# One block on one core: the output projection's second half reordered, the second norm's vectors loaded as columns, the planner's prices changed

## The chip, the cores and the metric

The kernel runs on 1 core of one Trainium2 chip. The metric is the device time of one execution in microseconds (us). Engines are named as in the profile: PE (TensorE, matrix products), DVE (VectorE), ACT (ScalarE), POOL (GpSimd), SP (SyncE, which here only issues transfers). Each engine runs its own list of instructions strictly in the order of the program, so an instruction that waits also holds everything behind it on that engine.

## What is computed

The reference is one block of an encoder on 512 rows of 1024 numbers, all in float32. Cut to what matters here:

```python
mod = silu(c) @ w_ada + b_ada
sh1, sc1, g1, sh2, sc2, g2 = split(mod, 6)
h = rms(x, norm1_g) * (1 + sc1) + sh1
z = h @ w_in                                   # 33 pieces of 128 columns
rec = hgrn2(...)                               # 4 recurrent heads of 128
att = dsa_attention(...)                       # 8 heads of 64: four pairs, 128 wide each
mix = concat([rec, att]) @ w_out               # the output projection, 1024 x 1024
x = x + g1 * mix
h2 = rms(x, norm2_g) * (1 + sc2) + sh2
logits = h2 @ [w_rg, w_re] + [b_rg, b_re]      # 20 columns: 4 groups, 16 experts
# each row goes to 2 of 16 experts: y = (silu(h2 @ w1) * (h2 @ w3)) @ w2
x = x + g2 * y
```

## The kernel before

A product of two float32 matrices is done as three products of split numbers: each operand is split into a high part (`wh`, `hx[..][:, 0]`) and a low part (`wl`), and `mm3` issues high by high, high by low, low by high. ACT casts the high part of each weight piece, and DVE (now and then POOL) subtracts it to get the low part.

**The planner.** The first part of the program, up to the experts, is not written in the order in which it runs. Every piece of work is a generator that is handed to `Desk` with a rank. The desk keeps an estimated clock for each engine, takes the generator that can begin first (in steps of 100 ns, then by rank), and lets it issue. `Engine.call` gives the estimated price of each instruction. So the prices set the order in which each engine's list is written. On the chip only that order is left: the estimates themselves delay nothing.

**The stages.** (1) `square_gen` squares the four pieces `xt` of x on ACT and adds them up on DVE in one sum `acc`; one float32 product with a matrix of ones gives the sums of squares of the first norm. `norm1_gen` multiplies eight chunks of w_ada by silu(c) for its vectors. (2) The 33 pieces of z are computed (`z_gen`) beside the recurrent heads, the indexer with its top-256 search (`topk_gen`), the four head pairs of attention (`attend_gen(j)`, j = 0 to 3), and the other six parts of mod: `ada_gen` goes through 64 loads `dd` in eight groups, sums each group on DVE (`acc`), turns it on PE and writes 512 numbers to the scratch `modD` in HBM. (3) `out_gen` is the output projection: half 0 takes the recurrent heads (tiles `mix` 0 to 3), half 1 the head pairs (`mix` 4 to 7). For each half there are two column halves c, four row tiles t, and per (c, t) two weight pieces p of two head tiles each, so 12 products per (c, t), 96 per half. The results stand in two PSUM banks of tag `z`. Half 1 begins only when all four head pairs are done; at that point the tiles of the attention are freed (`gp.close()`), the pool `mw` is opened in their place, and weight piece `NZ + 5` (half 1, c = 0, p = 1) is split into it. (4) `post_gen(t)` turns each finished row tile `xm[t]`, multiplies it by the router's weights `wr`, picks the experts and stores h2. `rows_gen` prepares the second norm: it loads sh2 and sc2 from `modD` as rows that are repeated on all 128 partitions (`sh2b`, `gs2b`), turns them on PE to columns (`shT`, `gsT`) and folds them into `wr` and the bias `cb`. (5) The 16 experts follow in an order that is written by hand: 12 weight pieces of 512 KB per expert come through a ring of 34 places, are split on ACT and DVE, and used on PE. SP issues their loads in order, each as soon as its place is free; the first eight wait for the end of `ada_gen`, since they use its memory.

In the names of the profile, `a`, `z`, `o`, `u` are PSUM banks, `nl` is an attention tile, `csm` holds the constant matrix of the head norm, and nearly every instruction has line L177, that of the planner's helper.

## Time and profile before

| | |
|---|---|
| median of 3 runs | 728.02 us (727.63 to 729.42) |
| the profiled execution | 727.48 us |
| its span, first to last instruction | 725.6 us |
| PE busy | 683.1 us (94%) |
| DVE busy | 630.9 us (87%) |
| ACT busy | 439.0 us (61%) |
| mean granted TensorE clock | 0.987 |

A busy PE in this profile is not a PE at its peak, since products overlap and their ends are modelled. The chain of work that ended last runs half of its time through PE, 21% through transfers and 14% through DVE. Times in the text are us from the start of the span.

### The profile page before, as it was taken

How to read it: one execution, taken by the hardware profiler on the slowest of the kernel's cores; microseconds unless marked ns; L12 is line 12 of the kernel's file. 1: busy time of each engine (PE TensorE's matmuls, PEld its weight loads, DVE VectorE, ACT ScalarE, POOL GpSimd, SP SyncE). 2: the span in 40 equal slices, each digit the busy share in tenths (PEclk: the TensorE clock that was granted, in tenths of full speed). 3: DMA queues.
4: the chain of work that ended last, by engine and by line, in shares of the span. 5: the costliest groups of instructions: out<-in, count | busy, mean ns of one | idle time of the engine just before them, and what ended most of it. 6: DMA issues, size and time to landing. Idle time of an engine off the chain costs nothing.

```text
span 725.6 us, 10941 instructions
## 1 busy us (share of the span) xinstructions
PE 683.1 (94%) x3794; PEld 530.9 (73%) x3794; DVE 630.9 (87%) x1057; ACT 439.0 (61%) x670; POOL 202.4 (28%) x104
## 2 busy tenths in 40 slices
PE   3999999999999999999889979999999999999993
PEld 1666778877778776667568858888888888888872
DVE  4637889999999987978866889999999999999991
ACT  4326664545557466553343458888777777777770
POOL 0120010001321321122200030165655655556412
PEclk9999999999999999999989999999999999999997
DMA  9947532231120324685697889999999999999502
GB/s 363 406 154 224 190 111 88 89 115 59 56 90 30 117 88 164 225 308 181 188 362 305 315 318 406 390 376 347 365 363 367 354 350 358 364 361 349 187 11 33
DMA packets 57388, 172.84 MB, mean 238 GB/s; under 512 B 11954, under 2 KB 12530, under 8 KB 56304
## 3 DMA queue, kind: packets, MB, share of 16 engines
q1 hardware_dynamic: 45168, 150.54, 56.1%
q0 software_dynamic: 10720, 17.24, 8.5%
q10 hardware_dynamic: 1440, 4.31, 1.5%
q8 instruction: 32, 0.52, 0.3%
q14 instruction: 28, 0.23, 0.1%
HBM read 167.50 MB, written 15.24 MB: 252 GB/s over the span
## 4 chain that ended last, share of the span: by engine, by line
PE 50%; DMA 21%; DVE 14%; issue 10%; ACT 3%; SPq 0%; POOL 0%; POOLq 0%; DVEq 0%; ACTq 0%
PE z L177 30%; PE a L177 14%; DMA w<-in_w_dram 13%; DVE wl L177 8%; DMA out_dram<-yo,idx 6%; PE u L177 2%; PE h L177 2%; PE o L177 2%; DMA dd<-in_w_ada_dram 1%; DMA chunk<-in_w_ada_dram 1%; DVE yo L177 1%; DVE xl L177 1%; DVE oh L177 1%; ACT wh L177 1%; ACT sq L177 1%
## 5 line engine op out<-in xcount | busy, mean ns | idle before, releaser
L177 ACT CAST wh<-w 128x1024 fp32r<-128x1024 f32 x168 | 174.5, 1054 | 44.2 <-PE h L177 30.9
L177 DVE TENSOR_TENSOR wl<-w,wh 128x1024 fp32r<-128x1024 f32 x168 | 196.6, 1216 | 2.4 <-ACT wh L177 2.0
L177 PE MATMUL z<-hx,wh 128*128 128x512 f32 x496 | 163.1, 409 | 1.1 <-DVE hx L177 0.6
L1358 POOL DMA_INDIRECT out_dram<-yo,idx x16 | 123.7, 7730 | 120.8 <-DVE wl L177 64.1
L177 PEld LDWEIGHTS z<-hx,wh 128*128 128x128 f32 x496 | 88.8, 189 | 27.1 <-issue 8.7
L177 PE MATMUL h<-wl,xh 128*128 128x512 f32 x256 | 101.4, 396 | 0.0
L177 PE MATMUL h<-wh,xh 128*128 128x512 f32 x256 | 100.8, 394 | 0.0
L177 PE MATMUL h<-wh,xl 128*128 128x512 f32 x256 | 100.6, 393 | 0.0
L177 ACT CAST wh<-raw 128x1024 fp32r<-128x1024 f32 x64 | 67.1, 1052 | 55.3 <-PE z L177 48.0
L177 PE MATMUL z<-hx,wl 128*128 128x512 f32 x248 | 97.6, 394 | 0.0
L177 DVE TENSOR_TENSOR wl<-raw,wh 128x1024 fp32r<-128x1024 f32 x64 | 81.6, 1286 | 6.8 <-ACT wh L177 6.5
L177 PEld LDWEIGHTS h<-wl,xh 128*128 128x128 f32 x256 | 48.5, 189 | 12.9 <-DVE wl L177 3.0
L177 PEld LDWEIGHTS h<-wh,xh 128*128 128x128 f32 x256 | 48.5, 189 | 10.2
L177 PEld LDWEIGHTS h<-wh,xl 128*128 128x128 f32 x256 | 48.4, 189 | 10.1 <-DVE xl L177 0.3
L177 PE MATMUL y<-wh,hh 128*128 128x512 f32 x128 | 53.0, 414 | 2.0 <-DVE yo L177 2.0
L177 PEld LDWEIGHTS z<-hx,wl 128*128 128x128 f32 x248 | 46.8, 189 | 10.3
L177 PE MATMUL y<-wl,hh 128*128 128x512 f32 x128 | 50.6, 396 | 0.0
L177 PE MATMUL y<-wh,hl 128*128 128x512 f32 x128 | 50.6, 395 | 0.0
L177 PE MATMUL z<-wh,mix 128*128 128x512 f32 x128 | 48.3, 421 | 0.0
L177 DVE SCALAR_TENSOR_TENSOR acc<-dd,cT,acc 128x512 f32<-128x512 f32 x56 | 43.8, 782 | 3.6 <-DMA dd<-in_w_ada_dram 3.0
L177 POOL TENSOR_TENSOR dd<-b 128x512 f32<-128x512 f32 (+1 forms) x14 | 17.2, 1242 | 93.5 <-PE a L177 79.0
L1353 POOL DMA_INDIRECT xe<-h2D,idx x15 | 17.1, 1140 | 80.5 <-DVE idx L177 46.3
(290 smaller groups left out, 1145.2 us busy)
## 6 DMA issues: line engine op xcount, KB each, us to landing
w<-in_w_dram SPq DMA_DIRECT2D x164, 512.0 KB
raw<-in_w_in_dram SPq DMA_DIRECT2D x33, 512.0 KB
dd<-in_w_ada_dram SPq DMA_DIRECT2D x64, 256.0 KB
raw<-in_w_dram SPq DMA_DIRECT2D x24, 512.0 KB
chunk<-in_w_ada_dram SPq DMA_DIRECT2D x8, 1024.0 KB
raw<-in_w_out_dram SPq DMA_DIRECT2D x8, 512.0 KB
lineR<-lineD POOLq DMA_DIRECT2D x4, 640.0 KB, 17.6
xt<-in_xT_dram SPq DMA_DIRECT2D x4, 512.0 KB
```

The source lines that it names most:

```text
L177: r = f(*a, **k)
L1353: pool.indirect_dma_start(out=dst, out_offset=None, in_=h2D, in_offset=bass.IndirectOffsetOnAxis(ap=ix, axis=0), bounds_check=T - 1, oob_i ...
L1358: pool.indirect_dma_start(out=out, out_offset=bass.IndirectOffsetOnAxis(ap=ix, axis=0), in_=y, in_offset=None, bounds_check=T - 1, oob_is_ ...
```

## The change

Four things are edited. The planner's prices are new: products, reads of PSUM, sums and DVE's three-operand instructions are priced higher. `square_gen` becomes four parts: DVE adds the two halves of each squared piece, and four products with ones add the pieces up in PSUM. The second norm's vectors are loaded from `modD` once more as columns (`shc`, `gsc`, 8 numbers on each of 128 partitions), so that the 16 turns, four ACT copies and two groups of bank use go; the repeated rows are still loaded, for h2. In `out_gen`, half 1 no longer waits for all head pairs: for each row tile it does the pieces p = 0 (`mix` 4 and 5) of both column halves first, in both banks, and then p = 1 (`mix` 6 and 7). Weight piece `NZ + 6` is split ahead of `NZ + 5` for that. Freeing the attention's memory becomes a generator of its own, `places_gen`.

```diff
             if self.name == "pe":
                 w = a[1]
                 if op == "transpose":
-                    cost = 107.0
+                    cost = 110.0
                 elif w.dtype == BF16:
-                    cost = max(0.4167 * n, 28.0)
+                    cost = max(0.4167 * n, 50.0)
                 elif o.shape[0] == 32:
-                    cost = 0.4167 * n
+                    cost = 60 + 0.3 * n
+                elif w.dtype == F32R:
+                    cost = 18 + 0.4167 * n
+                    if w.shape[0] == 64:
+                        cost = max(cost / 2, 70.0)
                 else:
-                    cost = max(0.4167 * n * (4 if w.dtype == F32 else 1), 213.0 * w.shape[0] * o.shape[0] / P ** 2)
...
+                    cost = max(1.95 * n, 225.0 * o.shape[0] / P)
...
-                    n = int(np.prod(a[1].shape[1:])) + 100 * ("accum_out" in k)
+                    n = int(np.prod(a[1].shape[1:])) + 220 * ("accum_out" in k)
...
                 cost = 60 + n * rate
+                if self.name == "act":
+                    cost += 50 if getattr(a[1], "space", None) == PSUM else 90
+                elif op in ("scalar_tensor_tensor", "tensor_tensor_reduce", "tensor_tensor_scan", "copy_predicated"):
+                    cost += 100
...
     def split_gen():
-        for n in range(len(stream)):
+        for n in [*range(NZ + 5), NZ + 6, NZ + 5, NZ + 7]:
...
+    def part_gen(i, ms):
+        sq = hd.tile([P, 2, T], F32, name="sqx", bufs=4)
+        yield [("xt", i)]
+        yield "act"
+        act.activation(sq, xt[i], AF.Square)
+        yield "dve"
+        dve.tensor_tensor(sq[:, 0], sq[:, 0], sq[:, 1], op=OP.add)
+        yield [("square", i - 1)] * (i > 0)
+        yield "pe"
+        pe.matmul(ms, ones, sq[:, 0], start=i == 0, stop=i == 3)
...
         yield ["ada_rows"]
         desk.at += 2500
+        for dst, r in ((shc, 2), (gsc, 4)):
+            pool.dma_start(dst, bass.AP(tensor=modD.tensor, offset=modD.offset + r * 512, ap=[[1, P], [P, KT]]))
+        at = desk.at + 2500
         mod_rows(gs2b, 4)
-        desk.at = mod_rows(sh2b, 2)
-        yield ["mw"]
-        yield "dve"
-        dve.scalar_tensor_tensor(gs2b, gs2b, 1.0, n2b, op0=OP.add, op1=OP.mult)
+        desk.done["norm rows"] = mod_rows(sh2b, 2)
+        desk.at = at
+        yield "dve"
+        dve.scalar_tensor_tensor(gsc, gsc, 1.0, V("n2g"), op0=OP.add, op1=OP.mult)
...
         pc, mo = yield from slot_bank(tag="o")
-        for kh in range(2):
...
-                for k in range(4):
-                    pe.transpose(pt[:, k], src[:, (4 * kh + k) * P:(4 * kh + k + 1) * P], ident)
-                yield "act"
-                act.copy(dst, pt.rearrange("p a b -> p (a b)"))
...
+        yield "pe"
+        for k in range(KT):
+            pe.matmul(pc[:, 0:20], shc[:, k:k + 1].to_broadcast([P, P]), wr[:, k], start=k == 0, stop=k == KT - 1)
+        yield "dve"
+        dve.tensor_tensor(wr, wr, gsc[:, :, None].to_broadcast([P, KT, 20]), op=OP.mult)
         dve.tensor_tensor(cb, pc[:, 0:20], rbb, op=OP.add)
         mark(mo)
+
+    def scale_rows_gen():
+        yield ["norm rows"]
+        yield "dve"
+        dve.scalar_tensor_tensor(gs2b, gs2b, 1.0, n2b[0], op0=OP.add, op1=OP.mult)
...
+    def places_gen():
+        nonlocal mw, sel, oh0, pair2
+        yield [("att", j) for j in range(4)]
+        gp.close()
+        mw = ctx.enter_context(tc.tile_pool(name="mw", bufs=1, reuse_waits="tile"))
+        mark("mw")
...
+        for t in range(4):
+            banks = []
+            for p in range(2):
+                for c in range(2):
+                    if p == 0:
+                        banks.append((yield from slot_bank(tag="z")))
+                    elif c == 0:
+                        spawn(post_gen(t), ("post", t), "post")
+                    o, mz = banks[c]
+                    yield from piece_mm(o, 1, c, p, t)
+                    if p:
+                        spawn(add_gen(1, c, t, o, mz), ("add", 1, c, t), "use")
```

Since the prices set the order, much of the lists of all engines moves. These are the places that matter below. First PE's list before, from the last head pair's sum of squares (`a<-sq,csm`; `d` is its second term) to the first products of half 1. All 96 products of half 0 stand ahead of it; a group of `ada_gen` (`acc`, `vc`) stands between.

```order
L177 MATMUL a<-sq,csm 128x512
L177 MATMUL a<-d_3474,csm 128x512
L177 MATMUL a<-acc,ones 32x128
L177 MATMUL a<-cs,vc 32x128
...
L177 MATMUL z<-wh,mix 128x512
L177 MATMUL z<-wl,mix 128x512
L177 MATMUL z<-wh,mix 128x512 x2
L177 MATMUL z<-wl,mix 128x512
L177 MATMUL z<-wh,mix 128x512
L177 MATMUL a<-cs,sh2b 128x128 x4
```

The same place in PE's list now. 84 products of the projection stand ahead of the sum of squares, 30 follow it before the first turn of a finished row tile (`a<-cs,xm`).

```order
L177 MATMUL a<-sq,csm 128x512
L177 MATMUL a<-d_3514,csm 128x512
L177 MATMUL z<-wh,mix 128x512
L177 MATMUL z<-wl,mix 128x512
L177 MATMUL z<-wh,mix 128x512 x2
L177 MATMUL z<-wl,mix 128x512
...
L177 MATMUL z<-wh,mix 128x512
L177 MATMUL a<-cs,xm 128x128 x4
L177 MATMUL z<-wh,mix 128x512
```

The last group of `ada_gen` and the turns of the norm's rows have left this place; 12 products of half 0 and the first 12 of half 1 stand behind the sum of squares instead.

DVE's list now, from the last head pair's scaling by its norm (`sq<-u,vc,sq`) on; `raw` times `g1b` and `wl` are the preparation of the last weight pieces, `xm` the sums of finished products.

```order
L177 SCALAR_TENSOR_TENSOR sq<-u,vc,sq 128x512
L177 TENSOR_TENSOR wl<-raw,wh 128x1024
L177 TENSOR_TENSOR xm<-xm,z 128x512
L177 TENSOR_TENSOR raw<-raw,g1b 128x1024
L177 TENSOR_TENSOR mix<-sq,mix 128x512
L177 TENSOR_TENSOR wl<-raw,wh 128x1024
L177 TENSOR_TENSOR raw<-raw,g1b 128x1024
L177 TENSOR_TENSOR xm<-xm,z 128x512
L177 TENSOR_TENSOR wl<-raw,wh 128x1024
```

Before, three sums `acc` and the scaling of `gs2b` stood among these; now the low part of `NZ + 6`, a sum and a scaling stand between the head pair and its `mix`.

POOL's list now, from the load of the router's bias to the end of `ada_gen`. `Wb` is the last head pair's bias table, `nl` its masked sums.

```order
L1121 DMA rbb<-in_rb_dram 128x20
L1122 DMA wr<-in_w_r_dram 128x160
L954 DMA Wb<-lineR 128x2x512
L1130 DMA shc<-modD 128x8x1
L1130 DMA gsc<-modD 128x8x1
L996 DMA gs2b<-modD 128x1024
L996 DMA sh2b<-modD 128x1024
L1038 DMA modD<-acc 4x128
L177 TENSOR_TENSOR nl<-Wb,negm 128x384 x2
```

The two column loads are new; the loads of the rows stood behind the first `nl` of this head pair before, and stand ahead of them now.

## Rows read from the trace of the kernel before

**Rows 1.** Busy time per engine in stretches of the span (PEclk: granted clock).

```profile
core 0: us, PE busy (x) PEld busy (x) DVE busy (x) ACT busy (x) POOL busy (x), PEclk, DMA share, GB/s
60.00:340.00 280.00, 277.09 (x1676) 211.38 (x1674) 254.24 (x527) 157.95 (x317) 43.41 (x43) 1.00 0.39 130
...
350.00:375.00 25.00, 19.02 (x126) 13.51 (x123) 19.55 (x30) 10.39 (x21) 2.43 (x7) 0.86 0.75 265
...
360.00:370.00 10.00, 5.07 (x33) 3.97 (x33) 7.01 (x9) 3.65 (x6) 1.27 (x5) 0.66 0.68 248
...
500.00:550.00 50.00, 50.00 (x246) 40.48 (x245) 50.00 (x60) 39.67 (x46) 27.42 (x7) 1.00 1.00 360
```

**Rows 2.** DVE's sums of the experts' results, and one wait between 450 and 650.

```profile
L177 DVE SCALAR_TENSOR_TENSOR yo<-y,wts,g2b x32: 729/742/753, 454.6 to 713.5; 128x512 f32<-128x512 f32 x32
...
ACT wh L177 <- DMA w<-in_w_dram: 0.5, 1, 0.5
```

**Rows 3.** PE in order of time, 357 to 379 (start, length, names, records; idle before, releaser).

```profile
357.01 0.45 PE L177 MATMUL a<-acc,ones 128*32 128x128 f32 x8
...
357.76 1.12 PE L177 MATMUL a<-sq,csm 128*128 128x512 f32 x2
358.82 1.12 PE L177 MATMUL a<-d,csm 2*128 2x512 f32 x2
364.94 0.68 PE L177 MATMUL a<-acc,ones 128*32 128x128 f32 x8 [4.99 <-DVE acc L177]
...
365.97 0.80 PE L177 MATMUL z<-wh,mix 128*128 128x512 f32 x1
...
370.81 0.97 PE L177 MATMUL o<-wr,shT 128*128 128x20 f32 x8
...
378.56 0.96 PE L177 MATMUL u<-wr,hT 128*128 128x20 f32 x8
...
403.85 0.39 PE L177 MATMUL z<-wh,mix 128*128 128x512 f32 x1
```

**Rows 4.** The chain of waits, 127 to 158: products back to back (start, length).

```profile
127.35 30.63 PE z L177 x135
```

**Rows 5.** DVE in order of time, 361 to 367.

```profile
361.33 0.75 DVE L177 SCALAR_TENSOR_TENSOR sq<-u,vc,sq 128x512 f32<-128x512 f32 x1 [1.15 <-ACT sq L177]
362.00 1.53 DVE L177 SCALAR_TENSOR_TENSOR acc<-dd,cT,acc 128x512 f32<-128x512 f32 x2
363.44 0.68 DVE L177 TENSOR_TENSOR mix<-sq,mix 128x512 fp32r<-128x512 f32 x1
...
364.71 1.22 DVE L177 SCALAR_TENSOR_TENSOR gs2b<-gs2b,n2b 128x1024 f32<-128x1024 f32 x1
365.84 1.22 DVE L177 TENSOR_TENSOR wl<-raw,wh 128x1024 fp32r<-128x1024 f32 x1
```

**Rows 6.** ACT, one cast of a weight's high part.

```profile
362.64 1.04 ACT L177 CAST wh<-raw 128x1024 fp32r<-128x1024 f32 x1
```

**Rows 7.** The start: PE, then ACT's last square and DVE's sum.

```profile
11.43 1.93 PE L177 MATMUL a<-chunk,cB 128*32 128x256 f32 x16 [11.43 <-DMA chunk<-in_w_ada_dram]
...
14.72 2.06 PE L177 MATMUL a<-accx,ones 128*128 128x512 f32 x2
16.71 1.94 PE L177 MATMUL a<-chunk,cB 128*32 128x256 f32 x16
...
5.07 2.18 ACT L177 ACTIVATE sqx<-xt 128x1024 f32<-128x1024 f32 x2
...
8.89 1.06 ACT L177 ACTIVATE sqx<-xt 128x1024 f32<-128x1024 f32 x1 [0.23 <-DMA xt<-in_xT_dram]
...
7.30 4.46 DVE L177 TENSOR_TENSOR accx<-accx,sqx 128x512 f32<-128x512 f32 x6
```

**Rows 8.** Transfers issued by POOL (KB each, median us to landing), and lineR's and Wb's landings.

```profile
lineR<-lineD POOLq DMA_DIRECT2D x4, 640.0 KB, 17.6
...
modD<-acc POOLq DMA_DIRECT2D x8, 2.0 KB, 3.1
...
wr<-in_w_r_dram POOLq DMA_DIRECT2D x1, 80.0 KB, 2.5
...
L524 POOL DMA_DIRECT2D lineR<-lineD x4: 1066/1072/1158, 41.6 to 44.9; - x4
...
DMA to landing us min/median/max: 4.0/10.6/18.9
```

**Rows 9.** SP's issues of the experts' first weights (start, time spent, count).

```profile
362.76 11.06 SPq L1064 DMA_DIRECT2D w<-in_w_dram  x12
374.80 6.27 SPq L1064 DMA_DIRECT2D raw<-in_w_dram  x4
381.95 57.44 SPq L1064 DMA_DIRECT2D w<-in_w_dram  x24
```

More of the change, by code (lines that the diff above doesn't have):

```diff
@@ L62 @@
 for _n, _w in (("c", 8), ("sc1b", 8), ("sh1b", 8), ("n1g", 8), ("lb0", 4), ("lb1", 4), ("recg", 4),
-               ("qg", 1), ("kg", 1), ("ikg", 1), ("ikb", 1), ("attg", 4), ("mod", 32)):
+               ("qg", 1), ("kg", 1), ("ikg", 1), ("ikb", 1), ("attg", 4), ("mod", 32), ("n2g", 8)):
     VEC[_n] = (_off, _off + _w)
@@ L407, in chunk_gen @@
                 desk.done["line0"] = desk.move(0.3)
+    def part_gen(i, ms):
[8 more added lines that the diff above has]
+        pe.matmul(ms, ones, sq[:, 0], start=i == 0, stop=i == 3)
     def square_gen():
-        acc = hd.tile([P, T], F32, name="accx")
+        ms, mb = yield from slot_bank()
         for i in range(4):
-            sq = hd.tile([P, 2, T], F32, name="sqx", bufs=2)
-            yield [("xt", i)]
-            yield "act"
-            act.activation(sq, xt[i], AF.Square)
-            yield "dve"
-            for j in range(2):
-                if i + j:
-                    dve.tensor_tensor(acc, sq[:, 0] if i == 0 else acc, sq[:, j], op=OP.add)
-        ms, mb = yield from slot_bank()
-        yield "pe"
-        pe.matmul(ms, ones, acc, start=True, stop=True)
+            spawn(part_gen(i, ms), ("square", i), "hx")
+        yield [("square", i) for i in range(4)]
         yield "act"
@@ L1109, in hymba_kernel @@
     hsq = mp.tile([P, 4, 2], F32, name="hsq")
+    gsc = mp.tile([P, KT], F32, name="gsc")
+    shc = mp.tile([P, KT], F32, name="shc")
     pool.dma_start(rbb, bass.AP(tensor=rb.tensor, offset=rb.offset, ap=[[0, P], [1, 20]]))
@@ L1149, in gate_gen @@
+    n2b = []
     def gate_gen():
@@ L1152, in gate_gen @@
         desk.at = mod_rows(g2b, 6)
+    sel = oh0 = pair2 = None
     h2s, routed, px = [None] * 4, {}, []
[L1156 to L1181 removed]
@@ new lines, in piece_mm @@
+    def piece_mm(o, half, c, p, t):
+        tt = slice(t * P, (t + 1) * P)
+        n = NZ + half * 4 + c * 2 + p
+        yield [("split", n)]
+        wh, wl = halves[n]
+        for k in range(2):
+            kt = 4 * half + 2 * p + k
+            yield [("mix", kt)]
+            mx = pair[kt]
+            kc = slice(k * 512, k * 512 + 512)
+            yield "pe"
+            mm3(o, mx[:, 0, tt], mx[:, 1, tt], wh[:, kc], wl[:, kc], p + k == 0, p + k == 2)
+        if t == 3:
+            mark(("used", n))
@@ L1182, in out_gen @@
+    def out_gen():
+        for c in range(2):
+            for t in range(4):
                 o, mz = yield from slot_bank(tag="z")
                 for p in range(2):
-                    yield [("split", n + p)]
-                    wh, wl = halves[n + p]
-                    for k in range(2):
-                        kt = 4 * half + 2 * p + k
-                        yield [("mix", kt)]
-                        mx = pair[kt]
-                        kc = slice(k * 512, k * 512 + 512)
-                        yield "pe"
-                        mm3(o, mx[:, 0, tt], mx[:, 1, tt], wh[:, kc], wl[:, kc], p + k == 0, p + k == 2)
@@ L1193, in out_gen @@
-                    if t == 3:
-                        mark(("used", n + p))
-                spawn(add_gen(half, c, t, o, mz), ("add", half, c, t), "use")
+                    yield from piece_mm(o, 0, c, p, t)
+                spawn(add_gen(0, c, t, o, mz), ("add", 0, c, t), "use")
+        for t in range(4):
+            banks = []
+            for p in range(2):
+                for c in range(2):
+                    if p == 0:
[6 more added lines that the diff above has]
+                        spawn(add_gen(1, c, t, o, mz), ("add", 1, c, t), "use")
@@ L1281, in scale_gen @@
     def scale_gen(t, h2):
-        yield ["rows"]
+        yield ["scaled rows"]
         yield "dve"
@@ L1308, in hymba_kernel @@
     spawn(gate_gen(), "gate", "rows")
+    spawn(scale_rows_gen(), "scaled rows", "rows")
     spawn(out_gen(), "out", "out")
+    spawn(places_gen(), "places", "load")
     spawn(first_gen(), "first", "first")
@@ L1677, in _layout @@
     put("mod", ba[2:6])
+    put("n2g", a["norm2_g"][0])
     f["vec"] = v
```

61 lines of the change are left out of this document (14 added, 47 removed).

## Prediction, made before the changed kernel ran

> **What bounds the kernel now.** I read four views. The stretches come first. From 60 to 340 PE is busy 277.1 of 280 us and DVE 254.2, so there is hardly any gap that a reader can point at. The stretch 350 to 375 is different: PE is busy 19.0 of 25 us and its granted clock is 0.86. In the experts both engines are full, as are the transfers [rows 1]. The second view is the order of time on PE around that hole. The last head pair's sum of squares starts at 357.76. PE is through with its two terms at about 359.9, and then waits 4.99 us for the last group of `ada_gen`. Half 1 of the projection begins at 365.97 [rows 3]. The hole also costs clock: in 360 to 370 the granted clock is 0.66, two thirds of the stretch at 1.2 GHz instead of 2.4 [rows 1]. The third view is DVE there: `mix` 7, which the last products need, was written at 364.12, between three sums `acc` [rows 5]. The fourth is the experts: their sums begin at 454.6 and the last comes at 713.5, a fixed rhythm, and between 450 and 650 ACT waited for a weight's transfer once, 0.5 us [rows 2]. So what the end of the projection gains, the experts can start earlier by, if their weights come earlier too. These start to load at 362.76: the first 16 follow each other, the next 24 take 57 us, because they wait for places that the projection frees [rows 9].
>
> **The change part by part.**
>
> *The hole, and half 1.* Call the start of the last sum of squares T (357.76 before). Before, 96 products stand ahead of T, and product 120, which finishes row tile 0, ends at 378.56, where the router's product starts: T + 20.8 [rows 3]. From there to the start of the last product, at 403.85, the lists hold the same work in both kernels: 72 products and the four tiles' turns and router products. So I work out when product 120 ends in the changed kernel. Back to back, products follow each other in 0.227 us (30.63 / 135) [rows 4]. 84 stand ahead of T. Behind T come the two terms, 2.2 us [rows 3], then 24 products, 5.4 us, that need nothing of the last head pair: T + 7.6. The next 6 need weight piece `NZ + 5`, and products 111 on need `mix` 7. DVE's list gives both, with the durations of rows 5: the scaling starts at T + 3.6 as before (361.33), 0.7; the low part of `NZ + 6`, 1.2; a sum, 0.6; `raw` times `g1b`, 1.2, to T + 7.3; `mix`, to T + 7.9. The high part of `NZ + 5` is cast on ACT behind that scaling, 1.04 [rows 6], to T + 8.3, and the low part comes to T + 9.6. PE thus waits about 2 us around T + 7.6 to 9.6. The same chain for `NZ + 7` (scaling, cast, a sum, low part: 1.2 + 1.1 + 1.2) ends at T + 13.1, and product 120 ends at T + 14.3. That is 6.5 us earlier than T + 20.8. No idle stretch of more than 2 us is left, so I count the clock as full. If DVE's chain hides wholly, product 120 ends at T + 11.9 (two terms 2.2, 36 products 8.2, the turns and a router product 1.5), a gain of 8.9; if each of DVE's five steps comes half a microsecond later, it is 4.
>
> *T itself.* PE's work ahead of T: 12 products go behind it (-2.7), the last group of `ada_gen` comes ahead of it (two sets of 8 records, 0.75 to the sum of squares [rows 3]), and the 8 column products come ahead of it; 4 such products of 20 columns took 0.97, so 1.9 [rows 3]. That is 0.0. DVE's work ahead of T grows: what stood behind the last scaling, three sums `acc` at 0.75 and the scaling of `gs2b` at 1.2, comes ahead [rows 5], 3.5 us, with small steps 4. DVE has idle time between 60 and 340 (25.8 of 280 us [rows 1]), but it is spread thin. Between 0 (all hidden) and +4 I take +1.5, nearer to hidden, since PE and not DVE is the fuller engine.
>
> *The squares.* Before, DVE's seven sums end at 11.76, PE starts with chunk 0 at 11.43 when it has landed, and the product with ones takes 1.99 (14.72 to 16.71) behind it. Now four such products, 8.0 us, stand ahead of chunk 0. With a square of 1.06 and a sum of 0.74, ACT's first square ends at 6.1 and its last at 9.95, so the first such product can start at 6.9 and the last not before 10.7. Back to back they end at 14.9: chunk 0 starts 3.5 us later, minus the 1.99 that is no longer behind it [rows 7]. At most +1.5 us; nothing, if the clock rises earlier because PE starts earlier. I take +0.5. The sums saved on DVE (three) lie in idle time there.
>
> *The columns.* Off PE and ACT go 16 turns and four copies, which are in T + 20.8 and not in T + 14.3, so they are counted already. On come two loads of 1024 single numbers each, issued by POOL, and the wait for them: `o<-wr,shc` stands on PE behind the sixth group of `ada_gen`, with everything of the last head pairs queued behind it; on DVE the multiplication of `gsc` stands ahead of head pair 2's scaling. Between that group and the product PE has 27 products (6.1), three square terms (3.2) and some 5.3 us of small products: 14.6 us. Against this run the write of `modD` (3.1 to land [rows 8], with ACT's copy and POOL's issue about 5), POOL's issue (about 1, as for `lineR` [rows 8]) and the landing. For that no row shows this form. The nearest below is the router's weights, 2.5 us; the nearest above by count of rows is `lineR`, 256 rows and 17.6 us with four in flight [rows 8]. Up to 8.4 us the wait is hidden. I take 6, near the lower end because there is one load ahead and not three, and so 0; the upper end is a rival below.
>
> The Trainium skill, page "DMA: Bandwidth & Descriptors", section "Rules for kernel authors", says that a transfer whose last dimension isn't contiguous becomes one descriptor per element, and advises against it. By that rule each column load is 1024 descriptors of 4 bytes. No run here shows such a load yet, and the page has no price for this case; the sum would be the same by it unless the landing passes the bound above.
>
> *The new prices.* They move places in all lists between 20 and 360 without adding work. The row that bounds what that can give is DVE's 25.8 us of idle time beside PE's 2.9 [rows 1]. What it can cost is not bounded by a row: I allow 6 us either way, a quarter of DVE's idle time, and take 0.
>
> *The experts* have the same lists. Their weights' first eight loads wait for `ada_gen`, whose last group now stands behind product 60 of the projection instead of 96; the others wait for places that the projection frees 4 to 6 us earlier. So I count nothing lost there.
>
> **Sum** against the profiled execution: 727.48 (span 725.6 and 1.9 around it) - 6.5 + 1.5 + 0.5 = 723.0. The median of the runs is 0.5 us above that execution; I forecast **723.3**.
>
> **The rivals.** (a) *The column loads hold PE.* If `shc` lands after 18.9 us, the slowest landing of `lineR` and `Wb` [rows 8], it is there 25 us after the group, PE stands 10.5 us, and the clock after such a gap costs about 3.4 more (the share 0.34 of 10 us lost in 360 to 370 [rows 1]): 723 + 14 = 737, slower. It decides from a landing of 8.4 us on, and turns the sign at about 12. For it: many small packets; against it: few other transfers run there. The rule of the Trainium skill given above speaks for it too. (b) *The order gives the gain back.* DVE's 4 us ahead of T come in full, the start costs 1.5, and the new order loses a few more: 727.5 - 6.5 + 4 + 1.5 = 726.5, up to 731. (c) *The order gains as well*: 6 us of DVE's idle time are used, 717. (d) *The weights don't come earlier.* The chain of the experts in rows 2 has hardly a wait for a transfer, yet transfers are at a share of 1.00 [rows 1]; if their stock sets the rhythm from the start, the whole gain is lost there: 728. Against it: the places are freed earlier by the same step [rows 9].
>
> **How the numbers follow.** Forecast (719 to 726.5) 0.48; (a) 0.12; (b) 0.14; (c) 0.16; (d) 0.10. About 0.3%, or 2.2 us, is what a measurement of this kernel can tell from no change: faster is below 725.8, slower above 730.2. Faster: 0.44 of the forecast, all of (c) and 0.06 of the others, 0.66. Slower: 0.09 of (a), 0.05 of (b), 0.01 of (d), 0.15. The rest, 0.19, is the same. The range 716 to 732 leaves out half of (a), and the far parts of (c) and (b).
>
> **What would show it.** Right: behind the last sum of squares PE runs 24 products without a gap, no idle stretch above 2 us there, and a granted clock of 1.00 through 350 to 375; the last product of the projection starts at T + 40 instead of T + 46; the experts' sums begin at about 450 and keep 17.3 us between the first and the next on average. T within 3 us of 357.8 shows that the prices did little. A gap on PE ahead of `o<-wr,shc`, or on DVE ahead of `gsc`, shows (a). ACT waiting on `w` in the first experts shows (d). If T moves by more than 5 us either way, the term of the prices was wrong.

## The result, and the profile after

The changed kernel takes 733.08 us (median of 12 executions, 729.69 to 737.27), the kernel before 727.92 on the same chip: a ratio of 1.0071, with a 95% interval of 1.0053 to 1.0089. It is slower, by 0.7%. The forecast was 723.3, range 716 to 732, so the sign was wrong too. The profiled execution took 730.2 us, with a span of 728.4, and is one of the faster ones of its kernel.

Set against the profile of before, the span grows by 2.8 us where I had summed up a gain of 4.5. The sums of products and of experts are taken from the order of time in both traces; "way" is used below for the third row.

| stretch | before | changed | difference | forecast |
|---|---|---|---|---|
| start to T, the last head pair's sum of squares | 357.76 | 362.09 | +4.3 | +2.0 |
| T to the start of the projection's last product | 46.1 | 39.0 | -7.1 | -6.5 |
| from there to the first expert product (the way) | 10.7 | 15.1 | +4.4 | 0 |
| from there to the first expert's sum | 40.1 | 39.7 | -0.4 | 0 |
| first expert's sum to the fifteenth's | 252.2 | 253.8 | +1.6 | 0 |
| fifteenth's sum to the end | 18.8 | 18.8 | 0.0 | 0 |

The stretches of the changed kernel, to be laid beside [rows 1] (busy time per engine, PEclk the granted clock):

```profile
core 0: us, PE busy (x) PEld busy (x) DVE busy (x) ACT busy (x) POOL busy (x), PEclk, DMA share, GB/s
15.00:25.00 10.00, 7.71 (x48) 4.58 (x48) 7.12 (x11) 4.52 (x7) 0.00 (x0) 0.66 1.02 419
60.00:340.00 280.00, 270.97 (x1662) 206.56 (x1662) 253.31 (x536) 156.46 (x314) 43.86 (x46) 1.00 0.42 143
260.00:340.00 80.00, 74.60 (x502) 51.66 (x501) 65.47 (x115) 41.59 (x94) 19.02 (x24) 1.00 0.67 234
350.00:375.00 25.00, 22.59 (x131) 15.22 (x129) 16.23 (x22) 9.96 (x17) 1.86 (x6) 1.00 0.94 356
360.00:370.00 10.00, 9.63 (x47) 6.46 (x42) 4.57 (x6) 3.54 (x6) 1.26 (x5) 1.00 1.02 400
```

The hole is closed: 360 to 370 has 9.63 us of PE work at a clock of 1.00, where before 5.07 us ran at 0.66. But 60 to 340, where the forecast saw no gap to speak of, has lost 6.1 us of PE's busy time, 4.4 of it in 260 to 340 (79.02 us before). PE in order of time, which answers to [rows 3]:

```profile
362.09 1.02 PE L177 MATMUL a<-sq,csm 128*128 128x512 f32 x2
...
364.09 0.50 PE L177 MATMUL z<-wh,mix 128*128 128x512 f32 x1
...
372.22 0.50 PE L177 MATMUL z<-wl,mix 128*128 128x512 f32 x1 [0.76 <-DVE wl L177]
...
376.30 0.96 PE L177 MATMUL u<-wr,hT 128*128 128x20 f32 x8
...
401.11 0.39 PE L177 MATMUL z<-wh,mix 128*128 128x512 f32 x1
401.34 0.60 PE L177 MATMUL a<-cs,xm 128*128 128x128 f32 x4
403.70 1.07 PE L177 MATMUL o<-wr,hT 128*128 128x20 f32 x8 [1.76 <-ACT hT L177]
404.61 0.64 PE L177 MATMUL a<-cs,xm 128*128 128x128 f32 x4
...
416.16 0.47 PE L177 MATMUL h<-wh,xh 128*128 128x512 f32 x1 [1.53 <-DVE pos L177]
```

Behind T it goes nearly as forecast: product 120 starts at 377.66, T + 15.6 (before T + 20.6, forecast some 14.1, since it was to end at 14.3), the longest wait is 0.78 us, the last product starts at T + 39.0. Then comes what the forecast did not see. The last row tile waits 1.76 us for ACT's copy `hT`, and the first expert product, to which the gain should have gone, waits 1.53 more. ACT and DVE there:

```profile
401.50 1.04 ACT L177 CAST wh<-w 128x1024 fp32r<-128x1024 f32 x1 [3.87 <-PE z L177]
402.46 0.63 ACT L177 ACTIVATE sc<-xm 128x512 f32<-128x512 f32 x1
403.08 0.56 ACT L177 COPY hT<-a 128x512 f32<-128x512 f32 x1
```

```profile
401.34 0.18 DVE L177 TENSOR_TENSOR em<-L,gm 128x16 f32<-128x16 f32 x1
402.58 1.23 DVE L177 TENSOR_TENSOR wl<-w,wh 128x1024 fp32r<-128x1024 f32 x1 [1.06 <-ACT wh L177]
403.72 0.68 DVE L177 TENSOR_TENSOR xm<-xm,z 128x512 f32<-128x512 f32 x1
```

The splits of the experts' weights (`CAST wh<-w`, `wl<-w,wh`) stand ahead of the last tile's copy and second sum `xm`, and wait for a place that the last product frees. That sum could have started at 401.5, when the last product ends, and starts at 403.72.

The experts, beside [rows 2]: DVE's sums and POOL's scatter of an expert's rows (ns least/median/most, first and last start).

```profile
L177 DVE SCALAR_TENSOR_TENSOR yo<-y,wts,g2b x32: 739/744/751, 455.8 to 717.9; 128x512 f32<-128x512 f32 x32
L1380 POOL DMA_INDIRECT out_dram<-yo,idx x16: 1542/2308/2374, 457.5 to 720.4; - x16
```

The sums span 262.1 us; in [rows 2] it is 258.9. The scatter's median is 2308 ns; before it is 9388. This pair of numbers becomes a fingerprint below.

### The profile page after: what moved, and what is told of

It is laid out like the page before. It is cut to its first block, busy times and chain, and to the rows that moved or that the text cites. A ratio compares the mean times of both kernels' runs of the same rounds, so it can differ in the third digit from the quotient of the medians.

```text
span 728.4 us, 10898 instructions
## 1 busy us (share of the span) xinstructions
PE 684.8 (94%) x3784; PEld 529.5 (73%) x3784; DVE 626.2 (86%) x1056; ACT 437.1 (60%) x666; POOL 113.1 (16%) x104
## 3 DMA queue, kind: packets, MB, share of 16 engines
q0 software_dynamic: 10784, 17.25, 8.6%
## 4 chain that ended last, share of the span: by engine, by line
PE 39%; DVE 25%; DMA 19%; issue 12%; ACT 3%; POOL 0%; POOLq 0%; DVEq 0%; SPq 0%; ACTq 0%
PE z L177 21%; DMA w<-in_w_dram 12%; PE a L177 12%; DVE wl L177 11%; DMA out_dram<-yo,idx 3%; DMA dd<-in_w_ada_dram 3%; PE h L177 3%; DVE m L177 2%; PE u L177 2%; PE o L177 2%; DVE scores L177 2%; DVE dd L177 1%; ACT wh L177 1%; DVE acc L177 1%; DVE oh L177 1%
## 5 line engine op out<-in xcount | busy, mean ns | idle before, releaser
L177 DVE TENSOR_TENSOR wl<-raw,wh 128x1024 fp32r<-128x1024 f32 x64 | 78.4, 1233 | 5.9 <-ACT wh L177 5.6
L1380 POOL DMA_INDIRECT out_dram<-yo,idx x16 | 36.2, 2260 | 126.0 <-DVE yo L177 119.2
L177 DVE SCALAR_TENSOR_TENSOR acc<-dd,cT,acc 128x512 f32<-128x512 f32 x56 | 46.7, 833 | 4.0 <-DMA dd<-in_w_ada_dram 3.5
L177 POOL TENSOR_TENSOR nl<-Wb,negm 128x384 f32<-128x384 f32 (+1 forms) x16 | 19.9, 1252 | 83.1 <-PE a L177 72.1
```

Of the source, the lines that this page charges most:

```text
L177: r = f(*a, **k)
L1380: pool.indirect_dma_start(out=out, out_offset=bass.IndirectOffsetOnAxis(ap=ix, axis=0), in_=y, in_offset=None, bounds_check=T - 1, oob_is_ ...
```

## The experiments

Every kernel was run together with the kernel before on the same chip; ratios are to that, with the 95% interval. T and the way are as above.

**What moved T: the prices, the order, or the columns?** The prices were taken out of the changed kernel (e1) and put alone into the kernel before (e2); the projection's order alone (e3) and the columns alone (e7) were put into the kernel before.

```
e1: -  cost = max(0.4167 * n, 50.0)            e2: the other way round,
    +  cost = max(0.4167 * n, 28.0)                in the kernel before
    ...  (all prices of the first hunk back)
e3: out_gen, places_gen, piece_mm and the order in split_gen, nothing else
e7: rows_gen with gsc and shc, scale_rows_gen, nothing else
```

> The changed kernel with only the planner's prices put back. T is the start of the last head pair's sum of squares (before 357.8, changed kernel 362.1). Theory P, the new prices cost the time between 60 and 340: T comes back by 3 us or more, to 359 or earlier, product 120 still ends at about T + 14, and the time falls from 733 to 729 or less. Rival O, the new order of the projection or the columns push T back, whatever the prices: T stays at 361 or later and the time within 1.5 us of 733.

> The kernel before with only the new prices. Theory P: T moves from 357.8 to 361 or later, with nothing gained behind it, and the time goes from 728 to 731 or more. Rival O: T within 1 us of 357.8 and the time within 1.5 us of 728.

> The kernel before with only the new order of the projection's second half (and of the weight pieces), old prices, old norm rows, old squares. The step of the forecast on the hole: product 120 ends at about T + 14 instead of T + 20.8 and the last product starts at about T + 39. If T stays within 1.5 us of 357.8 (theory P), the last product starts at 397 to 399 instead of 404; the time is then 723 if the way from the last product to the first expert product stays at 10.7 us, and 727 if that way grows to 15 as in the changed kernel. Rival O: T at 361 or later, time 730 or more.

> The kernel before with the norm vectors as columns only (16 turns and four copies go, two loads of single numbers come), all else as before. The step of the forecast: the loads are hidden, so T stays within 1 us of 357.8. With the turns gone, the rows of before that stand in the way of the first router product are gone too. If the columns alone shorten the hole, product 120 ends earlier than T + 20.8, by 2 to 4 us, and the time is 725. If the weights' scaling and splits on DVE and ACT set product 120 anyway, it stays at T + 19 to 21 and the time at 728.

| kernel | median us | ratio | T | T to the start of product 120 | way |
|---|---|---|---|---|---|
| e1 changed, old prices | 727.36 | 1.0004 (0.9983 to 1.0025) | 357.96 | 17.1 | 14.2 |
| e2 before, new prices | 735.04 | 1.0093 (1.0074 to 1.0111) | 362.18 | 18.1 | 14.7 |
| e3 before, new order | 734.37 | 1.0064 (1.0040 to 1.0088) | 360.63 | 16.1 | 16.2 |
| e7 before, columns | 737.34 | 1.0132 (1.0113 to 1.0150) | 357.73 | 21.3 | 10.9 |

PE at T in e1, then in e2:

```profile
357.96 1.02 PE L177 MATMUL a<-sq,csm 128*128 128x512 f32 x2
...
366.83 0.50 PE L177 MATMUL z<-wl,mix 128*128 128x512 f32 x1 [2.50 <-DVE wl L177]
```

```profile
362.18 1.02 PE L177 MATMUL a<-sq,csm 128*128 128x512 f32 x2
```

Theory P holds for T and the time: without the prices T is back to within 0.2 us of before, and the prices alone move it by 4.4. Its third part fails, since product 120 comes at T + 17 in e1 and not at T + 14. The prices cost some 5 us of the changed kernel: the ratios to the kernel before, 1.0071 and 1.0004, are 4.9 us apart, the medians 5.7 (733.08 and 727.36). The place is the end of the heads: from 260 to 340 PE is busy 79.20 us in e1, 74.60 in the changed kernel (above) and 76.49 in e2. What PE waits for between 60 and 345 (us in total, times, the longest) shows how: first the changed kernel's four largest, then e1's largest.

```profile
PE a L177 <- DVE dd L177: 3.0, 5, 0.9
PE a L177 <- ACT nl L177: 2.0, 1, 2.0
PE a L177 <- DVE acc L177: 1.9, 1, 1.9
PE u L177 <- DVE PT L177: 0.9, 1, 0.9
```

```profile
PE a L177 <- DVE dd L177: 1.1, 1, 1.1
```

With the smaller ones these waits are 8.5 us in the changed kernel and 2.5 in e1. The middle part begins 1.5 us earlier in the changed kernel (56.0 instead of 57.5), so T is 4.1 us later than in e1 and not 6. Which price put which of these instructions too late is not known. Windows of e1:

```profile
260.00:340.00 80.00, 79.20 (x539) 55.95 (x538) 68.19 (x121) 43.55 (x95) 18.33 (x21) 1.00 0.60 204
365.00:375.00 10.00, 6.53 (x22) 5.11 (x23) 7.45 (x10) 2.26 (x4) 0.00 (x0) 0.70 0.46 152
```

With the old prices the wait of 2.50 us for `wl` stands behind T, the granted clock falls to 0.70 there, and the hole is only half repaired. In the changed kernel twelve more products stand behind T and no wait reaches 0.8 us. Among all runs, no wait behind T reaches 0.8 us before product 120 only where PE's new prices and the new order come together, and T is 362 or later in each of them. A kernel with the closed hole and the early T was not found.

e3 and e7 were a surprise. Neither the order nor the columns gains anything alone; e3 loses 6.5 us, e7 9.4, which neither theory had. Both together, without prices and squares, are level with the kernel before (e16, below). In e3 all of half 0 and 12 products of half 1 stand ahead of T, which makes it late; product 120 comes earlier, but the wait of the hole is still there, 5.00 us against 4.99:

```profile
367.81 0.68 PE L177 MATMUL a<-acc,ones 128*32 128x128 f32 x8 [5.00 <-DVE acc L177]
```

In e7 it is gone, with the old order of products. So the columns (or the prices, e2) can move the last group of `ada_gen` off this place, and the new order, as I had read it, does not; nor do the columns always, since in e8 (below) the wait of 5.00 us is back. But with the old order e7 then has waits of 1.61 and 2.50 us behind T, product 120 comes no earlier than before, and the clock is low again and again:

```profile
360.00:380.00 20.00, 14.43 (x72) 10.00 (x63) 13.90 (x18) 6.51 (x11) 2.47 (x6) 0.66 0.52 176
```

Over 345 to 450 the clock takes 13.7 us from e7 and from e3 (sum of five-us windows, length times one minus the clock), 5.1 from the kernel before and 1.8 from the changed kernel.

**Which prices?** PE's alone back to old in the changed kernel (e8), then all but PE's (e12).

> The changed kernel with the old prices for PE's operations only, the new ones for ACT and DVE. If PE's prices are what delays T, T comes back to 358 to 359 and the time to 728; if ACT's and DVE's are, T stays at 361 or later and the time at 733.

> The changed kernel with the new prices for PE's operations only, the old ones for ACT and DVE (the opposite of the run in which T came at 375.8). If one group of the prices is what delays T, T is back at 358 to 359 here and the time at 728. If the two groups only work against each other, T is again later than the 362 of the changed kernel and the time above 733.

e8: 748.09, 1.0300 (1.0257 to 1.0343), T at 375.8. e12: 741.39, 1.0178 (1.0148 to 1.0207), T at 372.0. e8's time was in neither forecast; in e12 the rival came, the two groups working against each other. Half of the new prices is worse than all of them or none. No single group is to blame; the list that comes out is what counts, and it doesn't follow the prices in any simple way.

**What holds the way behind the projection?** The prices alone make it long (14.7 in e2), and so does the order alone (16.2 in e3), so no one edit is its cause. First the later splits were put behind the last tile's second sum (e4), then tiles 1 to 3 were given the old order of columns, with the new prices (e5) and the old (e6).

```
e4:  -  yield [("used", NZ + piece)]
     +  yield [("used", NZ + piece)] + [("add", 1, 1, 3)] * (piece > 4)
e5:  +  p, c = (a, b) if t < 1 else (b, a)      (in out_gen, half 1)
```

> The changed kernel, in which ACT and DVE split the expert weights that follow the first only after the last row tile's second sum is given out, so that they no longer stand ahead of that tile's copy and sum. In the changed kernel 15.05 us pass from the start of the projection's last product to the first expert product, before 10.7. Theory B, the splits in the wrong place hold the last tile: that way shrinks to 11 to 13 us, the first expert product comes 2 to 4 us earlier, and the time falls by as much, to 729 to 731. Rival W, the experts are bound by their weights' transfers and splits from the start: the first expert product comes earlier, but the first sum of an expert does not, and the time stays within 1 us of 733.

> The changed kernel, with the new order kept for row tile 0 of half 1 alone: tiles 1 to 3 do their left columns whole and then the right ones, as before. Theory B: in the changed kernel the last tile's left columns end 6 products before the end of the projection instead of 12, so both halves of its turn, copy and router product fall behind the projection, in a row. Then the way from the start of the last product to the first expert product falls from 15.05 us to 10.5 to 12, T stays at 362, and the first expert product comes at 411.5 to 413 instead of 416.2; the time falls by 3 to 4.5 us from 733, to about 729. Rival S: the way is long because the splits of the expert weights stand in it, in either order of the columns; it stays above 13.5 and the time within 1.5 us of 733.

> As the run before, with the old prices too: squares, columns and the early start of tile 0 are kept. If the two losses found so far (the prices, 4.3 us at T, and the end of the projection, 4.4 us) add up and nothing else is late, T is 357.9, the last product starts at about 400, the first expert product at 411 (before 414.5), and the time is 724, near the forecast's 723.3. Rival W: the experts' weights set the start; the first expert product comes early, the first sum of an expert not before 453, and the time stays at 727.

e4: 732.25, 1.0058 (1.0033 to 1.0084), way 14.0. The second sum starts at 401.58, as it should, but only 1.0 us of the 2.1 reaches the first expert product, because PE turns that half behind the first half's router product:

```profile
401.28 0.60 PE L177 MATMUL a<-cs,xm 128*128 128x128 f32 x4
402.71 1.07 PE L177 MATMUL o<-wr,hT 128*128 128x20 f32 x8 [0.84 <-ACT hT L177]
...
403.70 0.64 PE L177 MATMUL a<-cs,xm 128*128 128x128 f32 x4
...
415.09 0.47 PE L177 MATMUL h<-wh,xh 128*128 128x512 f32 x1 [1.53 <-DVE pos L177]
```

e5: 737.38, 1.0130 (1.0099 to 1.0161), way 16.4; e6: 735.21, 1.0099 (1.0084 to 1.0114), way 20.0. My theory that the order of the columns makes the way long was wrong; rival S, the splits, was nearer, though it had the time at 733. In e5 the split still stands ahead of the second sum, and in e6 PE waits 1.94 us for `sel`.

Then the waits named by the trace were taken out directly: splits later, both turns of the last tile ahead of its router products, another bank for the positions' product (e9); and, as a wait stayed, the experts' first two banks exchanged (e14).

```
e9:  +  if t == 3 and kh == 0: continue
     -  for k in range(4 * kh, 4 * kh + 4):
     +  for k in range(4 * kh if t < 3 else 0, 4 * kh + 4):
     +  bank()
        pn = bank([P, 4, 16])
e14: -  bank()
     +  pq.tile([P, 512], F32, tag="h1", name="h")    (ahead of the experts)
```

> The changed kernel with the three waits taken out that its trace shows behind the projection: the splits of the later expert weights come after the last tile's sums, PE turns both halves of that tile ahead of its router products, and the positions' product takes another bank than the first expert product. Theory B: with 0.5 us for the second sum, 2.4 for turn and copy, 2.4 for the router products and 7.0 from the router's sum L to the first expert product (as in the kernel before), the way from the last product to the first expert product is 11.5 to 13 us instead of 15.05, and the time falls by 2 to 3.5 us, to about 730. Rival: other steps come late in their place, the way stays above 14 and the time within 1 us of 733. T stays at 362 in both.

> As the run with three waits taken out, where the first expert product still waited 1.54 us, now with the first two banks of the experts exchanged. If that product waited for the readers of the bank in which it stands, the wait goes, the way from the last product to it falls from 13.6 us to 12.1, and the time by up to 1.5 us, from 731.4 to 730. If the wait has another cause it stays, and so do way and time.

e9: 731.38, 1.0036 (1.0015 to 1.0058), way 13.6, with the wait for `pos` still at 1.54: the bank of the positions' product was not its cause. e14: 730.05, 1.0022 (1.0003 to 1.0041), way 12.0:

```profile
404.92 0.39 PE L177 MATMUL z<-wh,mix 128*128 128x512 f32 x1
405.15 0.60 PE L177 MATMUL a<-cs,xm 128*128 128x128 f32 x4
406.19 0.65 PE L177 MATMUL a<-cs,xm 128*128 128x128 f32 x4 [0.43 <-DVE xm L177]
...
407.69 1.86 PE L177 MATMUL o<-wr,hT 128*128 128x20 f32 x16
...
416.89 0.48 PE L177 MATMUL h<-wh,xh 128*128 128x512 f32 x1
```

The wait is gone: the first expert product had stood in a bank that DVE was still reading. The way falls from 15.05 to 13.6 to 12.0, the ratio from 1.0071 to 1.0036 to 1.0022; the intervals of neighbours overlap, those of the first and the last don't. So 3.1 of the 4.4 us by which the way grew are these waits. Only half of it arrives: from the last product to the first expert's sum it is 50.7 us before, 54.7 in the changed kernel, 54.2 in e9 and 53.2 in e14. In e14's profile the granted clock is 0.73 over 425 to 430 and 0.59 over 430 to 435, in the changed kernel's 0.73 and 0.92.

**Why are the experts longer?** Of the kernels so far, those with the columns have a scatter of 2.3 us and 253.8 us from the first to the fifteenth sum, the others 9.4 and 252.2. First the columns' loads were moved to SP (e10, and e11 with both turns first), then the kernel before was given the columns' tiles and nothing of their work (e13), then the columns were put into memory that is given back before the experts (e17, the changed kernel).

```
e10: -  pool.dma_start(dst, bass.AP(tensor=modD.tensor, ...
     +  sp.dma_start(dst, bass.AP(tensor=modD.tensor, ...
e13: +  gsc = mp.tile([P, KT], F32, name="gsc")     (and shc; "n2g" in vec)
e17: -  gsc = mp.tile([P, KT], F32, name="gsc")
     +  gsc = heads.tile([P, KT], F32, name="gsc")  (and shc, and n2g's 8)
```

> The changed kernel with old prices (727.4), in which SP and not POOL issues the two column loads. In every kernel with the columns so far the experts take 1.5 to 3.1 us more from the first sum to the last (259.8 to 261.4 instead of 258.2) and POOL's scatter of an expert shows 2.3 us instead of 9.7. If the two more transfers on POOL's queue are the cause, the experts go back to 258.2 to 258.4 and the scatter to 9.7, and the time falls by about 1.5 us to 726. If it is the columns in another way, both stay as they are and so does the time.

> As the run before, and PE turns both halves of the last row tile ahead of its router products. With old prices the way from the last product to the first expert product was 14.2 us, with 1.5 us of a wait for the first half's copy and the second turn behind it. Theory B: the way falls to 12 to 13 us, the time by 1.5 us more than in the run before, to 724 to 725, which would be faster than both kernels. Rival: the clock or another wait takes it back, and the time is that of the run before.

> The kernel before with two more tiles of 32 bytes a partition and eight more constants, as the columns need them, but without the columns' work. If the layout makes the experts longer, they take 259.8 to 261.4 us from the first sum to the last and POOL's scatter shows 2.3 us; if the columns' work does it, they stay at 258.2 and 9.7. The time moves by the same 1.5 to 3 us in the first case, not at all in the second.

> The changed kernel, with the two small tiles and the eight constants put into the memory of the heads, which is given back before the experts, so that all that the experts use lies where it lay before. If the layout alone makes the experts longer, they take 258.2 us from the first sum to the last (changed kernel 261.4), POOL's scatter shows 9.7 us, and the time falls by about 3 us from 733, to 730. If not, both stay.

e10: 731.31, 1.0049 (1.0027 to 1.0071). The experts stay as they were, so POOL's queue is not the cause; SP's next loads `dd` come 4.2 us later instead (343.1, in e1 338.9). DVE's split at 343.73 takes 3.93 us beside POOL's `nl`, where in e1 it took 1.22 ahead of that; DVE is late with `PT`, PE waits 1.71 us for it at 348, and T is 360.05. e11: 731.27, 1.0034 (1.0020 to 1.0048): the way falls from 14.2 to 12.9 as expected, and the last product starts 1.3 us later, so nothing is left. e13: 730.79, 1.0039 (1.0021 to 1.0058), its experts:

```profile
L177 DVE SCALAR_TENSOR_TENSOR yo<-y,wts,g2b x32: 739/743/749, 456.1 to 718.2; 128x512 f32<-128x512 f32 x32
L1362 POOL DMA_INDIRECT out_dram<-yo,idx x16: 1542/2312/2375, 457.8 to 719.2; - x16
```

Two tiles of 32 bytes a partition and eight more constants, with no work but clearing the tiles once, bring the whole fingerprint: 2312 ns, and 253.8 us to the fifteenth sum. (The median rises by 3.3 us, of which the profile shows 1.6 in the experts.) And e17 takes it away:

```profile
L177 DVE SCALAR_TENSOR_TENSOR yo<-y,wts,g2b x32: 742/758/773, 467.6 to 726.6; 128x512 f32<-128x512 f32 x32
L1382 POOL DMA_INDIRECT out_dram<-yo,idx x16: 1542/9416/10859, 469.3 to 728.9; - x16
```

e17: 731.8, 1.0053 (1.0033 to 1.0073), 1.3 us less than the changed kernel, which by itself is within the noise. Its profiled execution, 738.25, is the longest of its twelve, with T at 369.95, so only its experts are read: 252.2 us to the fifteenth sum, as in e18 below. Layout it is, at 1.6 us of that stretch.

Where do the 1.6 us go? Here is one round of the kernel before, then the same of e13: ACT's casts, DVE's `hl`, and the splits behind it.

```profile
559.54 2.00 ACT L177 CAST wh<-w 128x1024 fp32r<-128x1024 f32 x2
560.53 0.68 DVE L177 TENSOR_TENSOR hl<-pt,hh 128x512 fp32r<-128x512 f32 x1
561.13 2.34 DVE L177 TENSOR_TENSOR wl<-w,wh 128x1024 fp32r<-128x1024 f32 x2
```

```profile
561.95 2.00 ACT L177 CAST wh<-w 128x1024 fp32r<-128x1024 f32 x2
562.39 0.68 DVE L177 TENSOR_TENSOR hl<-pt,hh 128x512 fp32r<-128x512 f32 x1
563.04 2.36 DVE L177 TENSOR_TENSOR wl<-w,wh 128x1024 fp32r<-128x1024 f32 x2
```

From the first sum of an expert to `hl` DVE takes 15.27 us in both. The split behind `hl` starts 0.60 us after it before and 0.65 in e13, where it starts 0.03 us behind the end of ACT's first cast (563.01; before, that cast had ended at 560.59, long ahead of the split). The cast stands behind PE's turn of the expert's `s`, which ends 14.3 us into the round instead of 13.75. A full round so takes about 18.20 us instead of 18.13. Twelve of them give 0.8 us; the thirteenth and fourteenth, 18.22 and 17.19 us instead of 17.65 and 16.95, give the other 0.8. Why PE is later in the round is not shown.

The last sum comes 6.0 or 7.6 us after the fifteenth in kernels of either layout; that step isn't explained.

**The squares, and the parts that gain.** e15 is e1 with both turns of the last tile first; e16 is e1 with the old squares; e18 is e15 with the columns in the heads' memory, as in e17.

> The changed kernel with old prices (727.4) and, for the last row tile alone, both turns ahead of the router products. Theory B: the way from the last product to the first expert product falls from 14.2 us to 12.9, T stays at 358, and the time comes to 726. Rival: the last step of the experts (6.0 or 7.6 us in the kernels so far) or the clock takes it back, 727 to 729.

> The changed kernel with old prices and the old squares: only the columns and the projection's order are left. If the new squares cost clock at 15 to 25 us, the granted clock there is 1.00 again instead of 0.73 and 0.58. The forecast's term of the squares is 0.5 us; with old prices the first product of the middle part came at 57.5 with either squares, so the transfers hide it: T stays at 358 and the time within 1 us of 727.4. If the squares cost time, T comes earlier by 1 us or more.

> The changed kernel with old prices, with both turns of the last row tile first (727.9), and the columns' tiles in the memory of the heads. The experts take 258.2 us instead of 259.8, and the time falls by 1.5 us to 726.4, just below the kernel before. If the transfers at the start or the clock decide instead, it stays at 727 to 728.

e15: 727.86, 0.9992 (0.9977 to 1.0007); the way is 12.9, but the profiled execution began 1.2 us later (first product of the middle part at 58.7 instead of 57.5), and the gain in the way is gone before the first expert's sum, which comes 53.4 us behind the last product in both: the granted clock over 425 to 430 is 0.66 in e15 and 1.00 in e1. The median is that of e1. e16: 727.78, 1.0007 (0.9986 to 1.0028), with T at 357.55. Its windows:

```profile
15.00:25.00 10.00, 9.51 (x49) 4.71 (x49) 6.55 (x11) 5.18 (x8) 0.00 (x0) 1.00 1.02 418
365.00:375.00 10.00, 7.00 (x23) 5.11 (x23) 7.03 (x10) 2.26 (x4) 0.00 (x0) 0.63 0.46 166
```

The new squares do lower the clock at 15 to 25 (0.66 in the changed kernel, 1.00 here), and it costs nothing that these runs can show: the transfers are the bound there, at a share of 1.02 in both.

e18: 725.63, **0.9976 (0.9967 to 0.9985)**. It is the one kernel that beats the kernel before, by 1.6 us, and with it the changed kernel (1.0071) by some 7 us:

```profile
L177 DVE SCALAR_TENSOR_TENSOR yo<-y,wts,g2b x32: 742/758/769, 456.2 to 716.7; 128x512 f32<-128x512 f32 x32
L1378 POOL DMA_INDIRECT out_dram<-yo,idx x16: 1542/9478/10872, 457.9 to 717.8; - x16
```

## Why the prediction was wrong, step by step

**T itself** failed. I gave the new prices 0, with 6 us either way, and DVE's added work 1.5. Measured: the prices 4.1 to 4.4 (e1, e2), with PE waiting 8.5 us instead of 2.5 between 60 and 345, and everything else 0.2 (e1). The bound was there, the value had no row behind it. I also wrote that a move of T above 5 us would show the term of the prices wrong, and one within 3 us that they did little; T moved by 4.3, between the two, and it was the prices all the same. A bound on a total does not test a term, a run of the term alone does.

**The hole and half 1** came out nearly right in size (product 120 gained 5.0 us of the 6.5, the last product 7.1), and partly for a wrong reason. The new order does not remove the wait for `ada_gen`'s last group (e3 keeps 5.00 us); the columns or the prices do (e7, e2). "No idle stretch of more than 2 us is left, so I count the clock as full" held for the lists I reasoned on, those of the changed kernel (0.78 us at most, clock 1.00). But it held through the prices that I had put at 0: with the old ones the wait is 2.50, and the clock falls to 0.63 to 0.70 (e1, e16).

**The experts** failed, in the sentence that nothing is lost there because their weights come earlier. The weights did come earlier (their first load is issued at 350.24 instead of 362.76), and neither ACT nor DVE waited for a transfer of theirs, so rival (d) is out. What was lost is the way: the splits that free weights allow stand in front of the last tile (e4, e9), and the first expert product lay in a bank still being read (e14); that is 3.1 of the 4.4 us of the way, of which 1.5 reach the first sum in e14, and what holds the rest stays open. I had followed the gain to the last product and not to the instruction that should inherit it.

**The columns** were hidden as forecast. The first load landed 4.8 us after its issue against my 6, and PE ran the 16 records of `o<-wr,shc` without a wait, so rival (a) is out. Their price was one that I had not looked for, 96 bytes of memory: 1.6 us in the experts (e13, e17).

**The squares** were given 0.5. With the old prices the first product of the middle part starts at 57.5 with the new squares (e1), at 57.1 with the old (e16) and at 57.5 in the kernel before; the start alone varies between 57.1 and 58.7 among the kernels with the old prices, so the term can't be told from 0.

**From the profile to the median** I added 0.5 us, as for the kernel before. In the changed kernel it is 2.9. Its six fastest executions (729.7 to 732.1) have a mean clock of 0.985 or 0.986, the six slowest (734.0 to 737.3) of 0.980 to 0.984. In which stretch the slower ones lost it isn't recorded; e1's, e3's and e7's profiles show such losses at the short waits between 360 and 420, which makes the same place likely here, not shown.

The misses add up: 2.3 at T, 4.0 from the last product to the first sum, 1.6 in the experts, 2.4 from profile to median, less 0.6 gained more in the projection, is 9.7 us between 723.3 and 733.08 (the forecast's own terms, 723.0 and 0.5, add up to 723.5). Rival (b) had the right kind of end (726.5 to 731), and in "the new order loses a few more" the step that came; but most of its sum was DVE's work in full and 1.5 us at the start, which both were next to nothing.

## What to carry to other kernels

An edit to a planner's prices is an edit to every list: run it alone first, and compare a few milestones, before anything is built on the new order; here it cost more than all the rest was worth. Follow a gain up to the instruction that should start earlier, and read what stands ahead of it on each engine, since work that waited for the same event comes free together with it. Small tiles that are used once can be put into memory that is given back, where they can't move what a long loop uses; that the old places were the faster ones is luck of this kernel.

## What the runs showed of the hardware

- The place of tiles in a partition's memory changes how long things take. 96 bytes make a full round of an expert 18.20 instead of 18.13 us, POOL's scatter 2.3 instead of 9.4 us, and the experts 1.6 us longer in all (e13 against before, e17 against changed). DVE's instructions are not what grows: its steps are the same up to `hl`. In its long form the scatter of the second to the twelfth expert ends 12.5 us behind the expert's first sum, whether it begins 1.7 or 3.6 us behind it; in its short form it ends 4.0 us behind it. The Trainium skill, page "SBUF — State Buffer", section "SBUF: two separate sides", says that GpSimd shares a port pair with DVE, that in some of DVE's modes, or with two inputs in SBUF against a GpSimd instruction that reads SBUF, the one that starts first holds it for the whole instruction, and that GpSimd can't write the descriptors of a transfer it issues while DVE holds it in a two-port mode. e10's split beside POOL's `nl`, 3.93 us instead of 1.22, may be such a case, though there the split began 0.55 us ahead of `nl`; no run tests it. The two scatters are not explained by the page, since DVE runs the same instructions in both, and no run here shows why 96 bytes should decide. That stays open.
- Behind a wait of 2.5 us on PE, with smaller ones after it, the granted clock went to its lower level, 1.2 instead of 2.4 GHz: e1's clock is 0.70 and e16's 0.63 over 365 to 375. Waits of 0.4 to 0.8 us in the changed kernel left it at 1.00 over 350 to 375. The length of one wait does not decide alone: in e1 a longer one left the clock at 1.00 over 420 to 435, in the changed kernel the clock behind the same wait (3.18 us) was 0.73 over 425 to 430.

```profile
425.03 0.25 PE L177 MATMUL pI<-pair,oh 128*128 128x5 bf16 x4 [3.17 <-DVE oh L177]
```

- A load of 1024 single numbers landed in 4.8 and 5.8 us in the changed kernel, in 4.0 and 3.1 in e1. The page of the profile counts 64 packets more on POOL's queue for the two of them (10784 against 10720). The Trainium skill, page "DMA: Bandwidth & Descriptors", section "Rules for kernel authors", says that such a transfer becomes a descriptor per element; the profile counts packets and no descriptors, so no run here decides that, but the price to fear was not there.
